# A hybrid decoder trunk on one core: batched merges of triangular inverses, one group for a pair's weighted sums, bias tiles as an input

## The chip, the cores and the metric

The kernel runs on one core of one Trainium2 chip. The metric is the time of the program on the device in microseconds (us), lower is better. Engines: TensorE (PE, its weight loads shown as PEld), VectorE (DVE), ScalarE (ACT), GpSimd (POOL) and SyncE (SP), which issues all DMA.

## What is computed

Two layers of a decoder trunk over 512 positions of width 1024, then a final RMSNorm. Each layer normalises its input, projects it once, feeds three groups of heads from the projection, multiplies each group's output with the SiLU of its own gate path, and adds one output projection to the residual. The parts that the change touches are the solve in the gated DeltaNet heads, the causal attention sweep, and the bias of the block-sparse (MoBA) heads:

```python
# gated DeltaNet, per head and chunk
L = jnp.where(strict, bc[..., :, None] * kk * decay, 0.0)
sol = lax.linalg.triangular_solve(L + jnp.eye(C), rhs, left_side=True, lower=True, unit_diagonal=True)
...
# latent attention and MoBA: softmax over past keys, weighted sum of values
p = jax.nn.softmax(logits, axis=-1)
return jnp.einsum('bhqk,bkhd->bqhd', p, v)
...
# MoBA: a T5 relative-position bias, by distance and head
rel_own = qpos[:, None] - kpos_own[None, :]
bias_own = t5_table[t5_bucket(rel_own)].transpose(2, 0, 1)[None]
l_own = jnp.einsum('bhqd,bhkd->bhqk', qi, kown) * scale
l_own = jnp.where(rel_own[None, None] >= 0, l_own + bias_own, -jnp.inf)
```

## The kernel before

The kernel's code does not issue instructions directly. `trace` (L514) records operations with the tiles that they read and write; `Plan.schedule` then runs a list scheduler with its own cost model, and `emit` writes every engine's instructions in the order found (all instructions therefore carry the line of `emit`, L485, and are told apart by their tiles). An operation's priority is its place in the recording plus a shift for its section (`TUNE`); a lower number goes first among the operations that are ready. The large projection products carry a further 1e6 (`FILL`), so that TensorE runs them only when nothing else is ready: they are called filler here. A tile takes a slot of a pool when its first operation is placed: 72 slots of 128x512 (`w`), which weights, attention tiles and others share, and 8 PSUM banks. A DMA load is placed only if ten `w` slots stay free, a weight split only if seven do. Operations inside `plan.group()` are placed as one, back to back on one engine. A `copy` goes to ScalarE or VectorE, whichever the planner finds first.

Weights come as pairs of 128x512 tiles: `wraw` is loaded, split into a high part `whi` on ScalarE and a low part `wlo` on VectorE or GpSimd, and a projection block (`fmajor`, L693) is 24 products into a PSUM bank `mm`, three for each slice of 128 rows; two split tiles make a block, so one tile of high and low parts serves 12 products. `mmt` are products with the other operand stationary (`tmajor`), the output projection among them.

**Inverses.** `N` holds L of all 4 heads, each with 4 double chunks of 128 (16 in all). Section `elim` (L934) inverts all 32x32 diagonal blocks at once on VectorE, by 31 steps over tiles of [128, 16, 32] (`row`, `xe`), to `x32` and its transpose `t32`. Section `inv` (L1204 to 1249) merges these to inverses of 64x64 blocks, head by head: a zeroed tile `X` [128, 4, 128] (`xinv`) and a zeroed `T64` [64, 4, 64]; four ScalarE copies of diagonal blocks; two GpSimd copies into `T64`; eight 32x32 products to `a2p`, two ScalarE copies to `a2`, eight products to `x12` (`x` in the trace), two signed VectorE copies into `X`, a transpose into `T64`; four 64x64 products to `a4p`, a copy to `a4`, four products to `x4p`, a signed copy into `X`, named `inv_done`. The products of a head wait for the `inv_done` of the head before. An fp32 product shows as two records. Then section `scan` of that head runs over its four double chunks: `sp` (three products on one bank), `u`, `st`, and the output `op`. Its inputs `vb`, `AT` and `qg` are made per head in section `vq` from two projection blocks.

**Attention sweep.** `attend` (L1067) is run for a pair of heads, four times in a layer. After the scores, it goes over four key blocks: for each, the weights `lg` of both heads are transposed on TensorE (`tp`) and copied to `pt`, and then a group of two products adds to `pv`, the two heads side by side in the columns of the array.

**Bias tiles.** In the first layer `t5_tiles` (L613) multiplies the 32-entry table by a one-hot array (`gdp`), scales it by 8 and fills the masked part (`gd`), writes it to DRAM (`gdd`), reads it back shifted by one per partition for each head (`hk`), turns it with an anti-diagonal (`tz`) and writes four tiles of 128x512 to DRAM (`gmd`). Both layers load these as `gmb` in MoBA's sweeps. The query is copied unscaled, and the score's scale of 0.125 is applied to the sum of score and bias.

Of the kernel before, what the change touches and what calls it, by code (L numbers as in the profile page):

```python
# [18 lines left out]
NEG = -1.0e30  # L19
# [470 lines left out]
def hybrid_trunk(  # L490
    ctx: ExitStack,
    tc: tile.TileContext,
    x_in, xt_in, ncol_in, final_norm_w, w_t1, w_v, w_f, w_o, w_uq, w_ukv, cols_in, adt_in, t5_table, trig_in, trigf_in,
    onehot_in, out,
# [12 lines left out]
          t5_table, trig_in, trigf_in, onehot_in, out)  # L507
# [6 lines left out]
def trace(plan, V, S, G, T, D,  # L514
          x_in, xt_in, ncol_in, final_norm_w, w_t1, w_v, w_f, w_o, w_uq, w_ukv, cols_in, adt_in,
          t5_table, trig_in, trigf_in, onehot_in, out):
# [87 lines left out]
    for i, j in ((0, 1), (1, 0), (2, 0), (3, 1)):  # L604
        G.memset(mask[32 * i:32 * i + 32, j:j + 1], 1.0)
    gmla = ct([P, 512], "gmla")
# [3 lines left out]
    gdd = plan.tile("dram", [4, 640], F32, "gdd")  # L610
    gmd = [plan.tile("dram", [P, 512], F32, f"gmd{h}") for h in range(4)]

    def t5_tiles():  # L613

        t5 = ht([32, 4], "t5")
        D.dma_start(t5, t5_table)
        onehot = wt([32, 512], "onehot")
        D.dma_start(onehot, onehot_in)
        gdp = g_bank("gdp")
        T.matmul(gdp[:4, :], lhsT=t5, rhs=onehot, start=True, stop=True)  # L620
        gd = wt([4, 639], "gd2")
        V.memset(gd[:, 0:127], NEG)
        V.tensor_scalar(gd[:, 127:639], gdp[:4, :], 8.0, None, op0=OP.mult)
        D.dma_start(gdd[:, 0:639], gd)
        anti = wt([P, P], "anti")
        G.memset(anti, 0.0)
        G.affine_select(anti, anti, pattern=[[1, P]], compare_op=OP.not_equal, fill=1.0,
                        base=-(P - 1), channel_multiplier=1)
# [143 lines left out]
    for l in range(L):  # L772
# [177 lines left out]
        inv_done = V.transpose(t32, x32)  # L950

        if l == 0:
            plan.section("t5")
            t5_tiles()
# [112 lines left out]
        def attend(q2, k2, gtiles, scale, v, pr, gate, ky):  # L1067
# [5 lines left out]
            for t in range(NT):  # L1073
# [7 lines left out]
                for hh in range(2):  # L1081
# [62 lines left out]
        for pr in range(2):  # L1144
# [29 lines left out]
            attend([[qs2[hh][half[hh]] for hh in range(2)], qs2], [[kh[half[hh]] for hh in range(2)], ks2], gmb, 0.125, vmb, pr, gate, 6 + pr)  # L1174
# [27 lines left out]

        for h in range(4):
            plan.section("inv")  # L1204

            X = wt([P, 4, P], "xinv")
            plan.after = [inv_done]
            G.memset(X, 0.0)
            T64 = wt([64, 4, 64], "t64")
            G.memset(T64, 0.0)  # L1210
            plan.after = ()
            for b in range(4):
                bs = slice(32 * b, 32 * b + 32)
                S.activation(X[bs, :, bs], x32[bs, 4 * h:4 * h + 4, :], AF.Copy)
            G.tensor_copy(T64[0:32, :, 0:32], t32[0:32, 4 * h:4 * h + 4, :])
            G.tensor_copy(T64[32:64, :, 32:64], t32[32:64, 4 * h:4 * h + 4, :])
            a2p = g_bank("a2p").rearrange("p (c i) -> p c i", c=4)
            plan.after = [inv_done]
            for c in range(NT):
                for q in range(2):  # L1220
                    a, b = slice(64 * q, 64 * q + 32), slice(64 * q + 32, 64 * q + 64)
                    T.matmul(a2p[b, c, 0:32], lhsT=N[h][a, c, b], rhs=t32[a, 4 * h + c, :], start=True, stop=True,
                             tile_position=(64 * q, 64 * q + 32))
            plan.after = ()
            a2 = ht([P, NT, 32], "a2")
            for q in range(2):
                b = slice(64 * q + 32, 64 * q + 64)
                S.activation(a2[b], a2p[b, :, 0:32], AF.Copy)
# [194 lines left out]
```

## Time and profile before

| | |
|---|---|
| median of 3 runs | 634.97 us (634.06 to 638.3) |
| the profiled execution, its own time | 637.48 us |
| its span, first to last instruction | 635.5 us |
| busy: TensorE, weight loads | 611.6, 493.1 us |
| busy: VectorE, ScalarE, GpSimd | 465.5, 361.9, 152.2 us |
| mean granted TensorE clock | 0.990 |
| instructions | 10493, of them 3488 matmul records |
| moved by DMA | 63.92 MB |

The profile is one execution. Times in it are microseconds from the first instruction. A busy share is covered time: matmuls overlap, so two that last 0.4 us each may start 0.23 us apart. Idle time of an engine is put down to what ended it.

### The profile page before, as it was taken

The numbers are of one execution on the slowest core, as the hardware profiler recorded it, in microseconds if no ns is written. First come the engines' busy times: TensorE is split into PE (matmuls) and PEld (weight loads), VectorE is DVE, ScalarE is ACT, GpSimd is POOL, SyncE is SP. The second block draws the span as 40 slices with busy tenths as digits, with TensorE's granted clock in tenths as the row PEclk, the third lists the DMA queues.
The fourth block names the chain that finished last, engine by engine and source line by source line (L and its number), as shares of the span: only waits on it lengthen the run. The fifth ranks groups of instructions, "written<-read, shape, count | busy, mean of one in ns | idle before, by whom it ended". The sixth has DMA issues, their size and how long they took to land.

```text
span 635.5 us, 10493 instructions
## 1 busy us (share of the span) xinstructions
PE 611.6 (96%) x3488; PEld 493.1 (78%) x3488; DVE 465.5 (73%) x1351; ACT 361.9 (57%) x948; POOL 152.2 (24%) x177
## 2 busy tenths in 40 slices
PE   8989999999999999999999899899999999999994
PEld 7767878877767887888898788688777688778884
DVE  6589878999857767734572888658999787786265
ACT  7887974624768545423455698447346976344032
POOL 2526503341403122000023141124402422030000
PEclk9999999998999999999999999989999999999998
DMA  8890341111123422350663112510012214214002
GB/s 313 301 331 18 116 131 51 51 50 51 52 67 118 134 68 96 101 195 0 195 214 114 57 45 85 166 34 1 18 51 84 67 68 150 76 57 166 0 35 100
DMA packets 36190, 63.92 MB, mean 101 GB/s; under 512 B 4644, under 2 KB 7428, under 8 KB 36136
## 3 DMA queue, kind: packets, MB, share of 16 engines
q1 hardware_dynamic: 36136, 63.26, 30.5%
q8 instruction: 27, 0.44, 0.3%
q14 instruction: 27, 0.22, 0.1%
HBM read 57.94 MB, written 5.30 MB: 100 GB/s over the span
## 4 chain that ended last, share of the span: by engine, by line
PE 62%; DVE 19%; ACT 8%; issue 5%; DMA 3%; POOL 2%; SPq 0%; POOLq 0%; ACTq 0%; DVEq 0%
PE mm L485 22%; PE mmt L485 19%; DVE row L485 6%; PE sp L485 3%; DVE xe L485 2%; PE tp L485 2%; PE pv L485 2%; PE op L485 2%; ACT n L485 1%; DVE mm L485 1%; DVE ks L485 1%; PE qkp L485 1%; DVE vs L485 1%; ACT lg L485 1%; DVE wlo L485 1%
## 5 line engine op out<-in xcount | busy, mean ns | idle before, releaser
L485 POOL TENSOR_TENSOR wlo<-wraw,whi 128x512 fp32r<-128x512 f32 x72 | 95.9, 1346 | 290.9 <-ACT whi L485 216.9
L485 PE MATMUL mm<-hy_hi,whi 128*128 128x512 f32 x384 | 155.1, 408 | 0.4 <-DVE vs L485 0.4
L485 PE MATMUL mm<-hy_lo,whi 128*128 128x512 f32 x384 | 154.9, 406 | 0.0
L485 PE MATMUL mm<-hy_hi,wlo 128*128 128x512 f32 x384 | 154.1, 406 | 0.0
L485 ACT ACTIVATE whi<-wraw 128x512 fp32r<-128x512 f32 (+1 forms) x152 | 88.7, 619 | 5.2 <-DMA wraw<-in_w_f_dram 4.4
L485 PEld LDWEIGHTS mm<-hy_hi,whi 128*128 128x128 f32 x384 | 72.9, 190 | 14.6 <-issue 1.3
L485 PEld LDWEIGHTS mm<-hy_hi,wlo 128*128 128x128 f32 x384 | 73.0, 190 | 14.0 <-issue 0.2
L485 PEld LDWEIGHTS mm<-hy_lo,whi 128*128 128x128 f32 x384 | 72.8, 190 | 14.0 <-issue 0.6
L485 DVE TENSOR_TENSOR wlo<-wraw,whi 128x512 fp32r<-128x512 f32 (+1 forms) x80 | 57.1, 738 | 3.2 <-ACT whi L485 3.1
L485 ACT ACTIVATE lg<-lg,nm 128x128 f32<-128x128 f32 (+3 forms) x64 | 35.3, 555 | 4.5 <-DVE nm L485 4.3
L485 PE MATMUL mmt<-whi,hy_hi 128*128 128x256 f32 (+1 forms) x128 | 34.4, 330 | 0.1
L485 PE MATMUL mmt<-wlo,hy_hi 128*128 128x256 f32 (+1 forms) x128 | 33.7, 324 | 0.0
L485 PE MATMUL mmt<-whi,hy_lo 128*128 128x256 f32 (+1 forms) x128 | 33.6, 323 | 0.0
L485 DVE STREAM_SHUFFLE row<-n 128x496 f32<-128x496 f32 (+30 forms) x62 | 28.9, 470 | 0.3
L485 DVE TENSOR_TENSOR xe<-xe,row 128x496 f32<-128x496 f32 (+30 forms) x62 | 26.2, 423 | 0.6
L485 PEld LDWEIGHTS mmt<-whi,hy_hi 128*128 128x128 f32 x128 | 24.5, 193 | 2.2 <-ACT whi L485 1.4
L485 ACT ACT_TABLE_LOAD x18 | 23.1, 1283 | 3.8 <-DMA ncol<-in_ncol_dram 3.5
L485 DVE TENSOR_TENSOR row<-row,xe 128x496 f32<-128x496 f32 (+30 forms) x62 | 25.0, 404 | 0.0
L485 PEld LDWEIGHTS mmt<-whi,hy_lo 128*128 128x128 f32 x128 | 24.1, 189 | 1.1 <-issue 0.7
L485 PEld LDWEIGHTS mmt<-wlo,hy_hi 128*128 128x128 f32 x128 | 24.6, 193 | 0.5
L485 DVE TENSOR_TENSOR mm<-mm,rrow 128x512 f32<-128x512 f32 x32 | 22.2, 693 | 3.8 <-PE mm L485 3.8
L485 PE MATMUL tp<-ident,lg 128*128 128x128 f32 x160 | 23.3, 277 | 0.0
(688 smaller groups left out, 1307.2 us busy)
## 6 DMA issues: line engine op xcount, KB each, us to landing
wraw<-in_w_f_dram SPq DMA_DIRECT2D x96, 256.0 KB, 3.5
wraw<-in_w_o_dram SPq DMA_DIRECT2D x32, 256.0 KB, 3.0
xt<-in_xt_dram SPq DMA_DIRECT2D x16, 256.0 KB, 4.7
wraw<-in_w_t_dram SPq DMA_DIRECT2D x16, 212.0 KB, 3.7
x<-in_x_dram SPq DMA_DIRECT2D x8, 256.0 KB, 4.9
wraw<-in_w_v_dram SPq DMA_DIRECT2D x8, 256.0 KB, 5.8
rb<-gcd SPq DMA_DIRECT2D x8, 256.0 KB, 4.7
y<-rd SPq DMA_DIRECT2D x16, 128.0 KB, 3.5
```

The lines of the kernel that those rows point to most:

```text
L485: o.insts.append(getattr(engines[o.eng], method)(*args, **kw))
```

## The change

Three edits. The merges of the inverses are recorded for all four heads at once, ahead of the first scan: `X` is one constant tile [128, 16, 128] and `T64` [64, 16, 64], zeroed once at the start and reused by both layers; each step handles 16 double chunks, its products in one group (two groups of eight where a bank holds eight), and copies into `T64` may go to ScalarE or VectorE instead of GpSimd. In `attend`, the transposes of all key blocks come first and the eight products into `pv` are one group. The bias tiles arrive as an input array in their final layout, so `t5_tiles` and its DRAM tiles go; the query is scaled by 0.125 when it is copied, and the score's scale becomes 1.

```diff
+    X = ct([P, 16, P], "xinv")
+    G.memset(X, 0.0)
+    T64 = ct([64, 16, 64], "t64")
+    G.memset(T64, 0.0)
...
-    gdd = plan.tile("dram", [4, 640], F32, "gdd")
-    gmd = [plan.tile("dram", [P, 512], F32, f"gmd{h}") for h in range(4)]
-
-    def t5_tiles():
...
-        T.matmul(gdp[:4, :], lhsT=t5, rhs=onehot, start=True, stop=True)
...
-        for h in range(4):
-            hk = wt([P, 512], "hk")
-            D.dma_start(hk, gdd.strided(h * 640, [[1, P], [1, 512]]))
-            tp = g_bank("tz")
-            with plan.group():
-                for b in range(4):
-                    T.transpose(tp[:, b * P:(b + 1) * P], hk[:, (3 - b) * P:(4 - b) * P], anti)
-            tz = wt([P, 512], "tz")
-            V.tensor_copy(tz, tp)
-            D.dma_start(gmd[h], tz)
...
+            pts = [[], []]
             for k in range(NT):
                 n = P * (NT - k)
-                pts = []
                 for hh in range(2):
...
-                    pts.append(pt)
-                with plan.group():
+                    pts[hh].append(pt)
+            with plan.group():
+                for k in range(NT):
                     for hh in range(2):
                         h = 2 * pr + hh
                         T.matmul(pv[hh * 64:hh * 64 + 64, k * P:], lhsT=v[k // 2][:, k % 2, h * 64:(h + 1) * 64],
-                                 rhs=pts[hh][:, :n], start=(k == 0), stop=(k == NT - 1), tile_position=(0, hh * 64))
+                                 rhs=pts[hh][k][:, :P * (NT - k)], start=(k == 0), stop=(k == NT - 1),
+                                 tile_position=(0, hh * 64))
...
-                S.activation(qs2[hh][half[hh]], p[half[hh]], AF.Copy)
+                S.activation(qs2[hh][half[hh]], p[half[hh]], AF.Copy, scale=0.125)
...
-                V.tensor_tensor(qs2[hh][other], p[own], qs2[hh][own].bitcast(F32), op=OP.subtract)
+                V.scalar_tensor_tensor(qs2[hh][other], p[own], 0.125, qs2[hh][own].bitcast(F32), op0=OP.mult, op1=OP.subtract)
...
-                gmb_done = [D.dma_start(g, gmd[2 * pr + hh])]
+                gmb_done = [D.dma_start(g, t5_in[2 * pr + hh])]
...
+        plan.section("inv")
+        low, high = (slice(0, 32), slice(64, 96)), (slice(32, 64), slice(96, 128))
+        for b in range(4):
+            bs = slice(32 * b, 32 * b + 32)
+            S.activation(X[bs, :, bs], x32[bs], AF.Copy)
+        for bs in (low[0], high[0]):
+            copy(T64[bs, :, bs], t32[bs])
+        a2p = g_bank("a2p").rearrange("p (c i) -> p c i", c=16)
+        with plan.group():
+            for i in range(16):
+                for a, b in zip(low, high):
+                    T.matmul(a2p[b, i, :], lhsT=N[i // 4][a, i % 4, b], rhs=t32[a, i, :], start=True, stop=True,
+                             tile_position=(a.start, b.start))
+        a2 = wt([P, 16, 32], "a2")
+        for b in high:
+            S.activation(a2[b], a2p[b], AF.Copy)
+        x12 = g_bank("x12").rearrange("p (c i) -> p c i", c=16)
+        with plan.group():
...
+        for a, b in zip(low, high):
+            V.tensor_scalar(X[a, :, b], x12[a], -1.0, None, op0=OP.mult)
+        V.transpose(T64[32:64, :, 0:32], X[0:32, :, 32:64])
+        a4 = []
+        for g in range(2):
+            p = g_bank("a4p").rearrange("p (c i) -> p c i", c=8)
+            with plan.group():
+                for i in range(8):
+                    T.matmul(p[64:128, i, :], lhsT=N[2 * g + i // 4][0:64, i % 4, 64:128], rhs=T64[:, 8 * g + i, :],
+                             start=True, stop=True, tile_position=(0, 64))
+            a4.append(wt([P, 8, 64], "a4"))
+            copy(a4[g][64:128], p[64:128])
+        for g in range(2):
+            p = g_bank("x4p").rearrange("p (c i) -> p c i", c=8)
+            with plan.group():
...
+            V.tensor_scalar(X[0:64, 8 * g:8 * g + 8, 64:128], p[0:64], -1.0, None, op0=OP.mult)
+
         for h in range(4):
-            plan.section("inv")
-
-            X = wt([P, 4, P], "xinv")
-            plan.after = [inv_done]
-            G.memset(X, 0.0)
-            T64 = wt([64, 4, 64], "t64")
-            G.memset(T64, 0.0)
...
-                T.matmul(sp[:, 1, :], lhsT=X[:, c, :], rhs=x1, start=True, stop=True)
+                T.matmul(sp[:, 1, :], lhsT=X[:, 4 * h + c, :], rhs=x1, start=True, stop=True)
```

The host's layout function builds the bias array by picking table entries by distance, with the mask's value where the key lies ahead.

## Rows read from the trace of the kernel before

**Rows 1.** The page's first part: busy time, share of span, instructions of each engine.
```profile
PE 611.6 (96%) x3488; PEld 493.1 (78%) x3488; DVE 465.5 (73%) x1351; ACT 361.9 (57%) x948; POOL 152.2 (24%) x177
```
**Rows 2.** The chain that ended last, merged pieces: start us, us, what.
```profile
91.28 2.30 PE pv L485 x16
...
302.49 16.71 PE mmt L485 x72
```
**Rows 3.** Timeline of TensorE, bias tiles: start, us, engine line op out<-in [idle before <-releaser].
```profile
23.65 1.02 PE L485 MATMUL gdp<-onehot,t 32*4 32x512 f32 x2
...
27.02 0.39 PE L485 MATMUL mm<-hy_hi,whi 128*128 128x512 f32 x1
...
30.90 0.40 PE L485 MATMUL mm<-hy_lo,whi 128*128 128x512 f32 x1
32.14 0.63 PE L485 MATMUL tz<-anti,hk 128*128 128x128 f32 x4 [0.84 <-DMA hk<-gdd]
...
37.25 0.48 PE L485 MATMUL mm<-hy_hi,wlo 128*128 128x512 f32 x1
```
**Rows 4.** Busy time by stretch: stretch, its length, engines (xcount), clock, DMA share, GB/s.
```profile
31.00:37.30 6.30, 3.30 (x22) 2.19 (x20) 5.38 (x18) 4.63 (x18) 5.52 (x7) 1.00 0.90 233
...
115.00:145.00 30.00, 27.85 (x143) 23.14 (x142) 29.35 (x76) 10.72 (x20) 12.74 (x10) 1.00 0.18 53
...
530.00:587.00 57.00, 56.63 (x325) 45.16 (x324) 42.84 (x124) 26.20 (x84) 9.00 (x7) 1.00 0.33 111
```
**Rows 5.** The same of tile wlo alone: PE, PEld, DVE, POOL.
```profile
17.00:31.00 14.00, 5.33 (x20) 3.76 (x20) 2.50 (x3) 6.59 (x4) 1.00 0.88 296
```
**Rows 6.** Timeline of TensorE, 191 to 196, one head's merges among filler.
```profile
191.32 0.40 PE L485 MATMUL mm<-hy_hi,whi 128*128 128x512 f32 x1
191.65 0.68 PE L485 MATMUL a4p<-t,N 64*64 64x64 f32 x8
192.25 0.50 PE L485 MATMUL mm<-hy_lo,whi 128*128 128x512 f32 x1
192.59 0.39 PE L485 MATMUL mm<-hy_hi,wlo 128*128 128x512 f32 x1
...
195.12 0.44 PE L485 MATMUL a2p<-t,N 32*32 32x32 f32 x16
195.49 0.50 PE L485 MATMUL mm<-hy_hi,whi 128*128 128x512 f32 x1
```
**Rows 7.** Tiles a2p and xinv: count, ns min/median/max, first and last start.
```profile
L485 PE MATMUL a2p<-t,N x128: 190/191/213, 167.8 to 526.8; 32*32 32x32 f32 x128
...
L485 ACT ACTIVATE xinv<-x x32: 292/306/312, 169.0 to 528.6; 32x128 f32<-32x128 f32 x32
...
L485 POOL MEMSET xinv<- x8: 518/524/532, 164.5 to 525.7; 128x512 f32 x8
```
**Rows 8.** Timeline of GpSimd, its first weight splits.
```profile
21.86 2.97 POOL L485 TENSOR_TENSOR wlo<-wraw,whi 128x512 fp32r<-128x512 f32 x2 [16.47 <-ACT whi L485]
```
**Rows 9.** Timeline of TensorE, a pair's weighted sums and what starts next.
```profile
173.99 1.08 PE L485 MATMUL pv<-pt,vmoba 128*64 128x512 f32 x4
175.03 0.65 PE L485 MATMUL a4p<-t,N 64*64 64x64 f32 x8
...
187.42 0.44 PE L485 MATMUL pv<-pt,vmoba 128*64 128x128 f32 x4
187.79 0.49 PE L485 MATMUL sp<-x,xinv 128*128 128x128 f32 x2
```
**Rows 10.** Waits of SP's queue: for what, us in total, times, longest.
```profile
SPq L485 <- PE tp L485: 41.8, 7, 23.2
```
**Rows 11.** Timelines in layer 1: the last inverse (VectorE), the last head's scan (TensorE).
```profile
535.72 0.42 DVE L485 TENSOR_SCALAR xinv<-x4p 64x256 f32<-64x256 f32 x1 [2.53 <-PE x4p L485]
...
566.51 0.38 PE L485 MATMUL sp<-vb,xinv 128*128 128x128 f32 x2
```

More of the change, by code (lines that the diff above doesn't have):

```diff
@@ L492, in hybrid_trunk @@
     tc: tile.TileContext,
-    x_in, xt_in, ncol_in, final_norm_w, w_t1, w_v, w_f, w_o, w_uq, w_ukv, cols_in, adt_in, t5_table, trig_in, trigf_in,
-    onehot_in, out,
+    x_in, xt_in, ncol_in, final_norm_w, w_t1, w_v, w_f, w_o, w_uq, w_ukv, cols_in, adt_in, t5_in, trig_in, trigf_in, out,
 ):
@@ L506, in hybrid_trunk @@
     trace(plan, V, S, G, T, D, x_in, xt_in, ncol_in, final_norm_w, w_t1, w_v, w_f, w_o, w_uq, w_ukv, cols_in, adt_in,
-          t5_table, trig_in, trigf_in, onehot_in, out)
+          t5_in, trig_in, trigf_in, out)
     plan.schedule()
@@ L515, in trace @@
           x_in, xt_in, ncol_in, final_norm_w, w_t1, w_v, w_f, w_o, w_uq, w_ukv, cols_in, adt_in,
-          t5_table, trig_in, trigf_in, onehot_in, out):
+          t5_in, trig_in, trigf_in, out):
     L = w_t1.shape[0]
@@ L609, in trace @@
                     fill=NEG, base=0, channel_multiplier=1)
-    gdd = plan.tile("dram", [4, 640], F32, "gdd")
-    gmd = [plan.tile("dram", [P, 512], F32, f"gmd{h}") for h in range(4)]
-    def t5_tiles():
[L615 to L619, printed above, removed]
-        T.matmul(gdp[:4, :], lhsT=t5, rhs=onehot, start=True, stop=True)
[L621 to L628, printed above, removed]
-        for h in range(4):
-            hk = wt([P, 512], "hk")
-            D.dma_start(hk, gdd.strided(h * 640, [[1, P], [1, 512]]))
-            tp = g_bank("tz")
-            with plan.group():
-                for b in range(4):
-                    T.transpose(tp[:, b * P:(b + 1) * P], hk[:, (3 - b) * P:(4 - b) * P], anti)
-            tz = wt([P, 512], "tz")
-            V.tensor_copy(tz, tp)
-            D.dma_start(gmd[h], tz)
     def copy(o, i, scale=None):
@@ L949, in trace @@
         t32 = wt([P, 16, 32], "t32")
[L950 to L954, printed above, removed]
+        V.transpose(t32, x32)
         plan.section("mlap")
@@ L1173, in trace @@
             plan.section("moba")
-            attend([[qs2[hh][half[hh]] for hh in range(2)], qs2], [[kh[half[hh]] for hh in range(2)], ks2], gmb, 0.125, vmb, pr, gate, 6 + pr)
+            attend([[qs2[hh][half[hh]] for hh in range(2)], qs2], [[kh[half[hh]] for hh in range(2)], ks2], gmb, 1.0, vmb, pr, gate, 6 + pr)
         plan.section("vq")
@@ new lines, in trace @@
+        a2 = wt([P, 16, 32], "a2")
[3 more added lines that the diff above has]
+        with plan.group():
+            for i in range(16):
+                for a, b in zip(low, high):
+                    T.matmul(x12[a, i, :], lhsT=a2[b, i, :], rhs=x32[b, i, :], start=True, stop=True,
+                             tile_position=(b.start, a.start))
+        for a, b in zip(low, high):
+            V.tensor_scalar(X[a, :, b], x12[a], -1.0, None, op0=OP.mult)
@@ L1252, in trace @@
+        for g in range(2):
+            p = g_bank("x4p").rearrange("p (c i) -> p c i", c=8)
+            with plan.group():
+                for i in range(8):
+                    T.matmul(p[0:64, i, :], lhsT=a4[g][64:128, i, :], rhs=X[64:128, 8 * g + i, 64:128],
+                             start=True, stop=True, tile_position=(64, 0))
+            V.tensor_scalar(X[0:64, 8 * g:8 * g + 8, 64:128], p[0:64], -1.0, None, op0=OP.mult)
+        for h in range(4):
             plan.section("scan")
@@ L1371, in _shape_constants @@
     bucket = np.where(n < 16, n, np.minimum(large, 31))
-    onehot = np.zeros((32, seq), np.float32)
-    onehot[bucket, np.arange(seq)] = 1.0
     cos, sin = trig[0].T, trig[1].T
     trigf = np.stack([np.tile(np.concatenate([cos, cos]), (4, 1)), np.tile(np.concatenate([-sin, sin]), (4, 1))])
-    return trig.reshape(2, 4, P, 16).transpose(2, 0, 1, 3), trigf, onehot
+    return trig.reshape(2, 4, P, 16).transpose(2, 0, 1, 3), trigf, bucket
 def layout(inp):
@@ L1389, in layout @@
     ukv = inp["mla_w_ukv"].reshape(L, P, 4, 128)
-    trig, trigf, onehot = _shape_constants()
+    trig, trigf, bucket = _shape_constants()
+    dist = 384 + np.arange(P)[:, None] - np.arange(512)[None, :]
+    t5 = np.where(dist >= 0, inp["t5_table"].T[:, bucket[np.maximum(dist, 0)]], np.float32(NEG))
     return {
@@ L1401, in layout @@
         "adt": np.stack([inp["gdn_A_log"], inp["gdn_dt_bias"]]),
-        "t5_table": inp["t5_table"],
-        "trig": trig, "trigf": trigf, "onehot": onehot,
+        "t5": t5.astype(np.float32),
+        "trig": trig, "trigf": trigf,
     }
```

39 lines of the change are left out of this document (removed).

## The prediction

> **What bounds the kernel now.** I read the page first, then the chain of work that ended last, then TensorE's order of work around each place that the change touches, then busy time by stretch. On the page TensorE is busy 96% of the span [rows 1]. "Busy" needs care, since matmuls overlap: what counts is how soon the next one can start. In the chain 72 matmuls on 512 columns take 16.71 us, 0.232 each [rows 2], and 14 filler products start one after another between 27.02 and 30.90, mostly 0.23 apart, while each lasts 0.40 [rows 3]. So I price TensorE by the distance from one start to the next, which I call a slot, and not by durations. By stretch [rows 4], TensorE is covered for 56.63 of 57 us in 530 to 587, where the last scans and sums run. There is one hole: between 31.0 and 37.3 it is covered for 3.30 of 6.30 us. The reader is to see an engine that always has a filler product to run (the planner puts the large products behind all other work), and therefore a kernel whose time is the sum of TensorE's slots. An instruction that goes saves its slot, if the filler behind it is there.
>
> **Bias tiles.** Sixteen transposes and one small product go, and with them four reads of 256 KB, four writes of as much, three small transfers and six VectorE operations. In [rows 3] the last filler product before the first transposes starts at 30.90 and holds its slot to 31.13; the next unbroken stretch begins at 37.25. In these 6.12 us three products ran (3 x 0.232 = 0.70): 5.42 us are the transposes and the waits ahead of them, 0.84 us in front of the first four. The small product at 23.65 holds about 0.9 us (two records, 1.02 with the tail of the last). Together 6.3 us. Is filler there to take the place? In 17 to 31 VectorE and GpSimd begin seven low halves of weights [rows 5]; leaving out two for work before it and work unfinished, five halves at 12 products each are 60, and 14 had started by 31. So yes. The low bound is that only the slots go and the waits return elsewhere: 4 x 0.38 + 0.9 = 2.4 (0.38 is what remains of the 0.63 of four transposes, less the tail that overlaps the next product). I take 6.3, since the supply is several times what the hole holds. SP's queue loses the four writes that wait for VectorE's copies of the transposes; what stood behind them, the weights of the latent projections among it, can only come earlier. The reads of the bias tiles by the block-sparse attention stay: same size, same queue, another source.
>
> **Inverses.** The same matmuls, 96 a layer, in 6 groups instead of 16. What a group costs beside its work is seen in [rows 6]: the product before it holds 0.33 (191.32 to 191.65) and the one behind it 0.34 (192.25 to 192.59) instead of 0.23, so 0.21 for the two edges. A group of 64x64 matmuls (eight records) holds 0.60 between them, a group of 32x32 ones (16 records) 0.37 (195.12 to 195.49). With edges that is 0.81 and 0.58; eight of each a layer, 11.1 us. After: four groups of 16 records hold at most 2 x 0.60 + 0.21 = 1.41 each, 5.6. The 32x32 records start (0.44 - 0.19) / 15 = 0.017 apart, with the 0.19 of one record [rows 7]; 64 of them hold 64 x 0.017 + 0.10 of drain + 0.21 = 1.4, two groups 2.8. That is 8.4 a layer, 2.7 saved, 5.4 in both layers. Bounds: 3, if the edges stay with the neighbours (other narrow work may then stand there); 9, if the drains of the 64x64 groups go too and those groups that are now interrupted pay no second edges. I take 6, near the value of the rows. The evictions shrink in number: 32 copies of diagonal blocks of 0.306 us on ScalarE [rows 7] become 8 of four times the width, 1.2 us each at the very most, so between nothing and 9.8 - 4.2 = 5.6 goes there. Copies into the transposed tile move from GpSimd to ScalarE or VectorE, four in all, each at most 1.2. All of it has TensorE's filler for cover; without it, the chain is a rival below. The two memsets go, once, to the start of GpSimd's queue, and GpSimd stands idle for 16.47 us before 21.86 [rows 8]: at 0.524 us for 512 elements [rows 7] both need some 3 us (3072 elements). No cost there; were GpSimd not idle, the first low halves would come these 3 us later.
>
> **Weighted sums.** Four groups of a pair become one. The 512-column group holds 1.04 us (173.99 to 175.03), the 128-column one 0.37 (187.42 to 187.79) [rows 9]: 384 columns are 0.67, so 0.15 of each group is fixed, and 0.21 of edges come to it. 24 groups go, 24 x 0.36 = 8.6, if all stood apart; they don't, for in the chain one whole pair runs unbroken in 2.30 us [rows 2], as one group of the new kind should (1280 columns, 2.23, and a drain). I take half, 4; bounds 2 and 6. The price is that eight transposed tiles live to the end of the sweep instead of two (a rival, below), and that the whole sum waits for the last copy; what stands behind it on TensorE is ordered by the planner to be filler.
>
> **Scale in the query copy.** ScalarE's copy takes a constant factor, VectorE's subtraction becomes multiply-and-subtract; eight of each. I price both at nothing, since neither reads or writes more. From above: were it a whole further pass, at 0.42 us for 256 columns [rows 11] some 0.84 each, VectorE would have 6.7 us more, which TensorE's filler covers, and which would be 6.7 us of time only where there is none; from below nothing.
>
> **Sum.** 6.3 + 6 + 4 = 16.3. The profiled execution took 637.48 us (span 635.5 and 2.0 around it), so 621.2; it stands 2.5 above the median of the runs, 634.97, and at the median's level this is 618.7. Forecast 619. Its own range: low terms 2.4 + 3 + 2 = 7.4, so 627.6; high terms 6.3 + 9 + 6 = 21.3, so 613.7, and some two less if the 2 MB of early transfers that go let later weights land sooner.
>
> **Rivals.**
>
> *The merged chain waits for its evictions.* Between its four products stand two 32-row copies, two signed copies and a transpose, two copies and two signed copies, each for the whole batch: with 0.306 us for 128 columns [rows 7] and 0.42 for 256 [rows 11] and no gain from width, 2.4 + 2.4 + 1.2 + 1.7 + 1.7 = 9.4 us a layer; half of that, with the fixed part paid once, is nearer. If TensorE stood idle for half, 4.7 a layer, 9.4 come back: 628. Against it: in [rows 6] TensorE runs filler right behind a group while the copy goes on. Chance 0.14.
>
> The Trainium skill speaks for this rival ("TensorEngine Tiling (Array Packing)", PSUM Bottleneck): tiling speeds up TensorE but not the copies out of PSUM, which may then become the limit. By that rule the inverse part brings nothing and the time would be 625 or above; by the rows the copies run beside filler, and the trace agrees with the rule only where filler is short.
>
> *VectorE's elimination gives part back.* In 115 to 145 VectorE is busy 29.35 of 30 us [rows 4], and the inverses cannot begin before it is done. If the time freed ahead of it (the bias tiles) only brings TensorE earlier to the end of its filler there, 6.3 come back: 625. Against it: what comes before the elimination is TensorE's work too, and moves with it. Chance 0.13.
>
> *Slower: weights starve.* Eight transposed tiles of 128x512 are held to the one group instead of two, six more out of a pool of 72 from which the weight tiles come too, and a load is not placed while fewer than ten would stay free. SP's queue already waits 41.8 us in 7 places for transposes to release a tile [rows 10]. If each of the eight sweeps holds weights back so long that TensorE has no filler for 5 us, 40 us come on top of 619: 659. It decides from some 2.8 us a sweep (22.6 us: the 16.3 and 1% of the time). For it: those waits. Against it: the inverses' tiles, two a head, leave that pool, and there are five halves of weights ahead in [rows 5]. Chance 0.12.
>
> That a late batch holds up the scans I leave out: the last inverse is ready at 536.13, and the last head's scan begins at 566.51 [rows 11], 30 us of cover.
>
> **How the numbers follow.** Forecast 0.60, the three rivals 0.14, 0.13 and 0.12, 0.01 for what I don't see. A measurement of this kernel can tell about 1%: the lines are 628.6 and 641.3. Faster: 0.60, most of the elimination's case and a little of the evictions' case, which lies on the line: 0.69. Within 1%: 0.19. Slower: 0.12. The range 611 to 634 leaves out the slower case and some 0.06 at its edges.
>
> **What would show it.** TensorE covered without a hole between 25 and 45 us: first term. One run of 64 small records for each of the two 32-wide products in a layer, and no idle time of several us around them: second. Unbroken runs of 16 records for the weighted sums, about 2.3 us long: third. It is wrong if the covered share of TensorE falls in the new trace where scans and attention stand, with waits for weight splits or for copies ahead of its work; or if its slots shrink as said and the span does not.

## The result and the profile after

| | before | after |
|---|---|---|
| median | 635.03 us (634.06 to 638.3) | 618.22 us (616.14 to 621.02) |
| ratio, 95% interval | | 0.9726 (0.968 to 0.9772) |
| profiled execution, its span | 637.48, 635.5 us | 618.93, 617.2 us |
| mean granted clock of it | 0.990 | 0.991 |
| moved by DMA | 63.92 MB | 61.72 MB |

The change saves 16.8 us, 2.7%. The forecast was 619.0, but two of its three terms were wrong, in opposite directions; most of this section and the next ones is about that. Runs more than 1.5% above the fastest of their kernel (one in e1, three in e10) are left out of the ratios.

From the page of after, to set beside [rows 1]: span and instructions, then busy time of each engine.

```profile
span 617.2 us, 10314 instructions
...
PE 592.1 (96%) x3470; PEld 488.4 (79%) x3470; DVE 462.0 (75%) x1315; ACT 354.6 (57%) x908; POOL 166.9 (27%) x161
```

TensorE is as full as before (96%), with 19.5 us less of covered time and 18.3 less of span. The distances from each matmul's start to the next add up to 624.7 us before and 606.1 after. That sum runs from the first start to the last and holds the waits too, so it follows the span by itself and proves nothing; it is of use only where it is split by tile, as further down.

Timeline of TensorE in after, layer 0's merges (compare [rows 6 and 7]): start, us, engine line op out<-in, form, records [idle before <-releaser].

```profile
172.48 1.20 PE L485 MATMUL a2p<-t,N 32*32 32x32 f32 x64
...
176.17 1.19 PE L485 MATMUL x<-x,a 32*32 32x32 f32 x62 [0.37 <-ACT a L485]
...
179.90 2.08 PE L485 MATMUL a4p<-t,N 64*64 64x64 f32 x32
181.92 1.11 PE L485 MATMUL x4p<-xinv,a 64*64 64x64 f32 x16
...
183.69 1.14 PE L485 MATMUL x4p<-xinv,a 64*64 64x64 f32 x16
```

The 64 records of each 32-wide product run together (those of `x` as 2 and 62, with a wait of 0.37 us between), both 64-wide groups of `a4p` back to back. The whole chain of layer 0 takes TensorE from 172.48 to 184.8; before, with four heads one after another, its products stood between 167.75 and 201.9.

The chain that ended last, after: start, us, what (compare [rows 2]).

```profile
85.92 2.31 PE pv L485 x16
...
188.47 2.30 PE pv L485 x16
...
205.19 2.31 PE pv L485 x16
```

The weighted sums of a pair run unbroken in all eight sweeps. And the start of the program, to set beside the first line of [rows 4], by stretch: length, busy PE, PEld, DVE, ACT, POOL (xcount), granted clock, DMA share, GB/s.

```profile
31.00:37.30 6.30, 6.30 (x30) 5.10 (x30) 6.16 (x24) 6.30 (x20) 4.12 (x5) 1.00 1.04 381
37.30:47.00 9.70, 6.74 (x33) 5.29 (x32) 9.35 (x34) 7.58 (x12) 5.69 (x5) 0.97 0.26 88
47.00:67.00 20.00, 18.09 (x87) 15.07 (x86) 14.72 (x32) 15.94 (x35) 10.17 (x8) 0.84 0.02 6
```

The last two stretches before:

```profile
37.30:47.00 9.70, 9.70 (x52) 7.93 (x51) 9.00 (x37) 9.03 (x16) 0.00 (x0) 1.00 1.04 392
47.00:67.00 20.00, 19.45 (x100) 15.27 (x98) 18.86 (x44) 16.15 (x33) 12.93 (x11) 1.00 0.20 68
```

The hole at 31 to 37.3 is closed: 6.30 of 6.30 us. But behind it there is a new one, 2.96 us without a matmul in 37.3 to 47, and in 47 to 67 the clock is granted at 0.84 of full speed on average, that is at half for some 6.3 of the 20 us. Before, both of these stretches had a clock of 1.00 and were covered for 9.70 of 9.70 and 19.45 of 20 us.

### The profile page after: what moved, and what is told of

It reads as the page before. It is cut to its first block, busy times and chain, and to the rows that moved or that the text cites. A ratio compares the mean times of both kernels' runs of the same rounds, so it can differ in the third digit from the quotient of the medians.

```text
span 617.2 us, 10314 instructions
## 1 busy us (share of the span) xinstructions
PE 592.1 (96%) x3470; PEld 488.4 (79%) x3470; DVE 462.0 (75%) x1315; ACT 354.6 (57%) x908; POOL 166.9 (27%) x161
## 2 busy tenths in 40 slices
DMA packets 34931, 61.72 MB, mean 100 GB/s; under 512 B 4448, under 2 KB 7232, under 8 KB 34880
## 4 chain that ended last, share of the span: by engine, by line
PE 67%; DVE 17%; ACT 7%; DMA 3%; issue 3%; POOL 1%; SPq 1%; ACTq 0%; POOLq 0%; DVEq 0%
PE mm L485 26%; PE mmt L485 18%; DVE row L485 5%; PE pv L485 3%; PE sp L485 3%; PE tp L485 3%; DVE xe L485 2%; PE op L485 2%; DMA wraw<-in_w_t_dram 2%; ACT n L485 2%; DVE qs L485 1%; PE kkp L485 1%; ACT whi L485 1%; ACT scr L485 1%; DVE kl L485 1%
## 5 line engine op out<-in xcount | busy, mean ns | idle before, releaser
L485 POOL TENSOR_TENSOR wlo<-wraw,whi 128x512 fp32r<-128x512 f32 x83 | 111.1, 1350 | 272.9 <-ACT whi L485 198.8
L485 PE MATMUL mm<-hy_hi,whi 128*128 128x512 f32 x384 | 150.4, 403 | 0.8 <-DVE qs L485 0.8
L485 PE MATMUL mm<-hy_lo,whi 128*128 128x512 f32 x384 | 149.8, 401 | 0.0
L485 PE MATMUL mm<-hy_hi,wlo 128*128 128x512 f32 x384 | 149.8, 402 | 0.0
L485 DVE TENSOR_TENSOR wlo<-wraw,whi 128x512 fp32r<-128x512 f32 (+1 forms) x69 | 51.5, 765 | 5.3 <-ACT whi L485 5.2
L485 POOL TENSOR_TENSOR ylo<-y,yhi 128x512 fp32r<-128x512 f32 x8 | 10.9, 1362 | 60.0 <-ACT yhi L485 60.0
L485 ACT ACTIVATE gate<-gate 128x512 f32<-128x512 f32 x16 | 10.1, 635 | 27.8 <-DVE gate L485 27.8
```

What stands on the lines that cost most here:

```text
L485: o.insts.append(getattr(engines[o.eng], method)(*args, **kw))
```

## The experiments

Each median is set against the runs of the kernel before beside it (635.2 to 635.4). First, every part by itself.

**e1_bias_only**: the bias tiles as an input and the scale in the query copy, nothing else.

```diff
-    def t5_tiles():
...
-                S.activation(qs2[hh][half[hh]], p[half[hh]], AF.Copy)
+                S.activation(qs2[hh][half[hh]], p[half[hh]], AF.Copy, scale=0.125)
...
-                gmb_done = [D.dma_start(g, gmd[2 * pr + hh])]
+                gmb_done = [D.dma_start(g, t5_in[2 * pr + hh])]
```

> Of the three edits only the bias tiles (with the query's scale). Slot theory (a kernel's time is the sum of TensorE's slots; filler takes what is freed): 6.3 us below before, about 628.7, and no hole between 31 and 37. Rival, the hole only moves (the freed 5.4 us of waiting come back as a wait for another operand in the same stretch): 2.4 below, about 632.6, with a new hole of several us before 70.

Measured: 632.45 us, ratio 0.9954 (0.9934 to 0.9974): 2.9 us, not 6.3. The hole has moved, as the rival said: TensorE, PE alone (busy, clock, DMA share, GB/s), and its longest wait.

```profile
17.00:67.00 50.00, 44.14 (x226) 1.00 0.52 183
```
```profile
45.29 0.52 PE L485 MATMUL latp<-ident,lt 128*128 128x128 f32 x3 [3.02 <-DVE lt L485]
```

**e2_inv_only**: the merges batched, nothing else. (The two constant tiles need room; the pool of small tiles has 54 instead of 56, here and in e5, e6, e9 and e11.)

```diff
-        for h in range(4):
-            plan.section("inv")
...
+        plan.section("inv")
+        low, high = (slice(0, 32), slice(64, 96)), (slice(32, 64), slice(96, 128))
```

> Of the three edits only the merged inverses (with two small tiles fewer, so that the constants fit). Slot theory: 6 us below before, about 629, bounds 3 and 9. Rival, the merged chain waits for its evictions: within 1 us of before, with idle time of TensorE ahead of the products of the merge. Rival, the order: one change of the program gives another plan for everything, and the time moves by some us in either direction, whatever the slots do.

Measured: 621.21 us, ratio 0.9774 (0.9752 to 0.9796): 14.2 us, more than twice the forecast, and outside its bounds of 3 to 9. TensorE's timeline shows that the products run as they do in after:

```profile
175.55 1.20 PE L485 MATMUL x<-x,a 32*32 32x32 f32 x64
179.07 2.05 PE L485 MATMUL a4p<-t,N 64*64 64x64 f32 x32
180.97 2.14 PE L485 MATMUL x4p<-xinv,a 64*64 64x64 f32 x32
```

**e3_pv_only**: the group of a pair's weighted sums, nothing else.

```diff
+            pts = [[], []]
             for k in range(NT):
...
-                with plan.group():
+            with plan.group():
+                for k in range(NT):
                     for hh in range(2):
```

> Of the three edits only the weighted sums in one group. Slot theory: 4 us below before, about 631, bounds 2 and 6. Rival, eight held tiles starve the weights: above before, with TensorE waiting for weight splits in the sweeps.

Measured: 632.19 us, ratio 0.9958 (0.9941 to 0.9975): 3.2 us, forecast 4. The three parts alone sum to 20.3 us, together they bring 16.8.

**e4_replan**: the kernel before, with one constant of the planner's cost model moved, so that the same operations come out in another order. It asks how much a new order alone moves the time.

```diff
-LAT_SAME = {"PE": 0.0, "DVE": 115.0, "ACT": 130.0, "POOL": 100.0, "SP": 0.0}
+LAT_SAME = {"PE": 0.0, "DVE": 117.0, "ACT": 130.0, "POOL": 100.0, "SP": 0.0}
```

> The kernel before with one number of the planner's cost model changed (2 ns in VectorE's latency to itself): the same operations, another order on every engine. Slot theory: within 1.5 us of before, since the slots are the same. Rival, the order: it moves by 3 us or more, and then single parts of a few us can't be told from a new plan.

Measured: 635.71 us, ratio 0.9995 (0.9976 to 1.0014). One draw is not a distribution, but 14.2 us is far above what reordering alone did here. For parts of 3 us one draw is too little: e7 and e9 below, which change only an order and where two tiles lie, come out 2.2 and 2.5 us slower, so a new order may be worth nearly as much as e1 or e3.

**e11_without_bias**: the change without its bias part (merges and sums only). By e2 and e3 the two should bring 17.3.

```diff
-    x_in, xt_in, ncol_in, final_norm_w, w_t1, w_v, w_f, w_o, w_uq, w_ukv, cols_in, adt_in, t5_in, trig_in, trigf_in, out,
+    x_in, xt_in, ncol_in, final_norm_w, w_t1, w_v, w_f, w_o, w_uq, w_ukv, cols_in, adt_in, t5_table, trig_in, trigf_in,
+    onehot_in, out,
...
-                gmb_done = [D.dma_start(g, t5_in[2 * pr + hh])]
+                gmb_done = [D.dma_start(g, gmd[2 * pr + hh])]
```

> The change without its bias tiles: merged inverses and the weighted sums in one group. By the parts alone (14.2 and 3.2) 617.6 if they add up, and then the bias tiles bring nothing to the whole change, which is at 618.2. If the bias tiles bring their 2.9 in the whole change too, 621.

Measured: 616.17 us, ratio 0.971 (0.9683 to 0.9736): 19.0 us, more than the 17.3 of the two parts. That is 2 us below the full change by the medians; the intervals overlap (after: 0.968 to 0.9772). So in the full change the bias part brings nothing that can be measured.

Why not? In after's trace VectorE, in 42 to 46 us, shows what TensorE's wait hangs on:

```profile
42.52 2.29 DVE L485 SCALAR_TENSOR_TENSOR kl<-kpp,mask,kh 64x512 fp32r<-64x512 f32 x3
44.82 1.27 DVE L485 TENSOR_SCALAR lt<-lt,rl_y 128x256 f32<-128x256 f32 x5
```

and TensorE, the last product before the hole and the first behind it:

```profile
41.96 0.39 PE L485 MATMUL mm<-hy_lo,whi 128*128 128x512 f32 x1
45.31 0.52 PE L485 MATMUL latp<-ident,lt 128*128 128x128 f32 x3 [2.96 <-DVE lt L485]
```

The last product ends at 42.35; the next work in TensorE's order, the transposes of `lt`, waits until VectorE has made `lt`, and VectorE runs three subtractions `kl` (2.29 us) first. Before, `lt` came first there, 1.4 us earlier:

```profile
43.38 1.91 DVE L485 TENSOR_SCALAR lt<-lt,rl_y 128x256 f32<-128x256 f32 x8
45.32 1.53 DVE L485 SCALAR_TENSOR_TENSOR kl<-kpp,mask,kh 64x512 fp32r<-64x512 f32 x2
```

Two experiments follow this up.

**e7_late_bias**: the kernel before, with the bias tiles' section of lower priority, so that their transposes come later.

```diff
-        "mlap": -224.9, "inv": 1348.7, "decay": -382.7, "t5": 149.2, "out": -161.4,
+        "mlap": -224.9, "inv": 1348.7, "decay": -382.7, "t5": 900.0, "out": -161.4,
```

> The kernel before with the section of the bias tiles put later in the planner's order (shift 900 instead of 149.2), so that their transposes don't stand in front of filler while their reads are under way; the slots stay. By the prediction's first term the waits, 3.9 us of the 6.3, go: about 631.5. Rival, the hole only moves to the next operand that is late in the first 70 us: within 1 us of before.

Measured: 637.62 us, ratio 1.0038 (1.0016 to 1.0059), 2.2 us slower. By stretch, PE alone (busy, clock, DMA share, GB/s):

```profile
17.00:31.00 14.00, 10.48 (x51) 1.00 0.97 331
31.00:37.30 6.30, 6.30 (x20) 0.73 0.63 192
```

The hole of [rows 4] is gone from 31 to 37.3, and 3.52 us of hole stand in 17 to 31 instead, with a slow clock behind it. Most of that hole is still the bias part's own: its small product waits for its one-hot operand.

```profile
30.54 1.01 PE L485 MATMUL gdp<-onehot,t 32*4 32x512 f32 x2 [2.17 <-DMA onehot<-in_onehot_dram]
```

So e7 does not show where the hole goes when the bias part's waits are gone; e1 does.

**e12_bias_order**: the full change, with one dependence more: the `kl` subtractions may not start before `lt`'s chain (`lat_done`) is through.

```diff
+            plan.after = [lat_done]
             V.scalar_tensor_tensor(kl[h][half], kpp[half], m, kh[h][half].bitcast(F32), op0=OP.mult, op1=OP.subtract)
+            plan.after = ()
```

> The changed kernel, with VectorE's four subtractions of the rotary keys held until the latent transposes are done. In the changed kernel three of them stand in front of the scaling of the latents, and TensorE waits 2.96 us for that at 42 to 45. If that wait is what the bias tiles' term lacks: some 3 us below the changed kernel, 615. Rival, the next operand is late instead, or the new order costs elsewhere: 618 or above.

Measured: 615.51 us (614.59 to 616.53), ratio 0.9689 (0.9667 to 0.9712): 2.7 us below after by the medians, the fastest version tried; the intervals overlap, and e11's too. TensorE over the whole stretch 17 to 67 us in before, after, e11 and e12, in this order (busy, clock, DMA share, GB/s):

```profile
17.00:67.00 50.00, 46.45 (x232) 1.00 0.65 215
```
```profile
17.00:67.00 50.00, 44.47 (x210) 0.93 0.48 172
```
```profile
17.00:67.00 50.00, 46.43 (x236) 1.00 0.66 221
```
```profile
17.00:67.00 50.00, 46.84 (x229) 0.97 0.54 183
```

Uncovered time plus what the clock falls short of full speed, an estimate from these lines: 3.55 us before, 5.53 + 0.07 x 50 = 9.0 after, 3.57 in e11, 3.16 + 0.03 x 50 = 4.7 in e12. The slots of the bias part's own matmuls, which e11 has and the others of the change have not, are 2.5 us in the trace of before. So this stretch should make after 9.0 - 3.57 - 2.5 = 2.9 slower than e11 (medians: 2.05), and e12 1.4 faster (0.7). The clock's part of this comes from one execution each: after's four runs have mean granted clocks of 0.984 to 0.996 and e11's six 0.984 to 0.994, so the two kernels don't differ in it. Without it the waits alone say the same: over the whole span after is uncovered for 25.1 us, e11 for 20.9 and e12 for 21.1, and 4.2 - 2.5 = 1.7 us is near the 2.05 by which e11 is below after. What e12 gets is not a closed hole: it waits too, now for a gate's operand, 2.85 us at 40 to 43. What it avoids is what came behind: in 47 to 67 it is covered for 19.91 of 20 us at 0.97.

```profile
43.17 0.37 PE L485 MATMUL gp<-gg,tri 128*128 128x16 f32 x2 [2.85 <-DVE gg L485]
```

Second, what makes the merges worth 14.2 us? Three candidates besides the groups: the wide copies, the constant tiles, and that the heads no longer wait for one another.

**e5_narrow_groups**: e2 with the products grouped by head, 16 groups a layer, copies as wide as before.

```diff
-        with plan.group():
-            for i in range(16):
-                for a, b in zip(low, high):
+        for h in range(4):
+            with plan.group():
+                for i in range(4 * h, 4 * h + 4):
+                    for a, b in zip(low, high):
```

> The merged inverses alone, as in the run with only that edit, but TensorE's products stand in groups of one head again (16 groups a layer instead of 6); the copies and signed copies between them stay as wide as the batch. Slot theory: the 10 groups more cost their drains and edges, 2.7 us a layer by the working of the prediction, so 5 to 6 of the 14.2 us come back: about 627. Rival, the count of copies: what the edit brings beyond 5.5 us comes from fewer instructions on ScalarE, VectorE and GpSimd, so little of the gain goes: about 622 to 624. Rival, the batch: heads no longer wait for one another's merges, 621.

Measured: 621.87 us, ratio 0.9792 (0.9759 to 0.9825), 13.5 us. The edit did not do what it was for:

```profile
168.99 1.20 PE L485 MATMUL a2p<-t,N 32*32 32x32 f32 x64
...
176.54 1.20 PE L485 MATMUL x<-x,a 32*32 32x32 f32 x64
```

Where nothing else is more urgent, the planner puts the four groups back to back anyway. So it says that the recording of one group is not needed; on what edges cost it says nothing.

**e6_narrow_copies**: e2 with one group for each step, and each copy cut into pieces of one head (those into `T64` on GpSimd again).

```diff
         for b in high:
-            S.activation(a2[b], a2p[b], AF.Copy)
+            for c in range(0, 16, 4):
+                S.activation(a2[b, c:c + 4], a2p[b, c:c + 4], AF.Copy)
```

> The merged inverses alone, with one group of products a step as in the edit, but every copy, signed copy and transpose between them is cut into parts of one head again (46 instructions a layer instead of 15), and the copies into the transposed tile go to GpSimd as before. Slot theory: the products' slots are as in the edit, so 621. Rival, the count of copies: the gain beyond 5.5 us goes, about 629.

Measured: 622.87 us, ratio 0.9802 (0.977 to 0.9834), 12.5 us. Narrow copies cost at most a microsecond or two. In tile `a2p`'s lines of e6 and of after (ns min/median/max) they are 16 of 258 ns against 4 of 590:

```profile
L485 ACT ACTIVATE a<-a2p x16: 252/258/270, 171.9 to 491.0; 32x128 f32<-32x128 f32 x16
```
```profile
L485 ACT ACTIVATE a<-a2p x4: 588/590/590, 174.9 to 491.1; 32x512 f32<-32x512 f32 x4
```

**e9_constant_tiles**: the kernel before, with `X` and `T64` as slices of constant tiles zeroed once, head by head otherwise.

```diff
-            X = wt([P, 4, P], "xinv")
-            plan.after = [inv_done]
-            G.memset(X, 0.0)
...
+            X = XC[:, 4 * h:4 * h + 4, :]
+            T64 = TC[:, 4 * h:4 * h + 4, :]
```

> The kernel before with one thing of the merged inverses alone: the inverses and their transposed tiles are constant tiles, zeroed once at the start; the merges still run head by head, each after the one before, with narrow products and copies. Theory A, the gain beyond the products' own slots comes from the tiles (no memsets in GpSimd's queue that wait for a free tile, eight tiles more for weights): 5 us or more below before, under 630. Theory B, it comes from the products of all heads being ready at once: within 2 us of before.

Measured: 637.71 us, ratio 1.0031 (1.001 to 1.0052). The constant tiles alone bring nothing: this kernel is 2.5 us slower, by them or by the new order.

**e10_heads_first**: the kernel before, with the merges of all heads recorded ahead of the scans and not waiting for one another, but neither batched nor grouped.

```diff
+        first_done = inv_done
         for h in range(4):
...
-            plan.after = [inv_done]
+            plan.after = [first_done]
...
+        for h in range(4):
             plan.section("scan")
```

> The kernel before with the merges of all four heads recorded ahead of the scans and no longer waiting for one another; tiles, memsets, products and copies stay as before, one head each. Theory A (the tiles): within 2 us of before. Theory B (ready at once, so that TensorE finds another head's products where it waited for a copy): most of the 14 us of the merged form, 622 to 626.

Measured: 668.23 us by the median of all six runs (658.24 to 671.91, mean granted clock 0.941 to 0.961), ratio 1.045 (1.0394 to 1.0507), that is 29 us by the runs counted there. TensorE in e10, 180 to 215 us (the profiled execution is the longest of the six): the heads' products mix record by record, TensorE runs out of other work, waits, and then is covered without a gap at half clock.

```profile
180.19 0.22 PE L485 MATMUL a2p<-t,N 32*32 32x32 f32 x2
180.21 0.22 PE L485 MATMUL x<-x,a 32*32 32x32 f32 x3
...
183.24 0.31 PE L485 MATMUL x<-x,a 32*32 32x32 f32 x8 [0.87 <-ACT a L485]
184.51 0.65 PE L485 MATMUL a4p<-t,N 64*64 64x64 f32 x4 [0.95 <-DVE vs L485]
```
```profile
180.00:184.00 4.00, 2.00 (x64) 1.00 0.30 80
...
188.00:212.00 24.00, 24.00 (x103) 0.50 0.18 56
```
```profile
180.00:215.00 35.00, 32.49 (x224) 0.56 0.24 76
...
510.00:560.00 50.00, 46.95 (x353) 0.73 0.17 55
```

The clock's shortfall in the last two stretches is 0.44 x 35 + 0.27 x 50 = 28.9 us, in a profiled span that is 34.4 longer than the one of before; there the granted clock was 1.00 in 180 to 215 and in 510 to 560. So e10 does not price its edit by itself: most of its loss is clock, and what it would take at full clock was not measured. It shows only that letting the heads' merges mix, record by record, did not bring the gain.

Last, is TensorE the bound, as all of this assumes?

**e8_more_products**: the full change, with a fourth product per slice in the gates' projections (the low part of the weight by the low part of the input, a term that the reference does not need): 64 more on 512 columns, 64 x 0.232 = 14.8 us of slots.

```diff
+            if B_GZ <= b:
+                T.matmul(p, lhsT=lo, rhs=hy_lo[:, k, :], start=False, stop=False)
```

> The changed kernel with 64 more products of 512 columns on TensorE (the product of the two low parts in the eight gate blocks of the DeltaNet heads), a known load of 64 x 0.232 = 14.8 us of slots as filler. Slot theory: 14.8 us above the changed kernel's 618.2, so 633. Rival, TensorE has room (its weight loads are busy 79%): less than half of it, under 626.

Measured: 633.61 us (631.03 to 639.39), ratio 0.999 to before (0.9958 to 1.0021): 15.4 us more than after by the medians, 14.6 by the profiled spans.

```profile
PE 608.2 (96%) x3534; PEld 501.0 (79%) x3534; DVE 463.1 (73%) x1324; ACT 356.9 (56%) x908; POOL 157.5 (25%) x154
```

A microsecond of slots added as filler is a microsecond of time, to within the some 3.5 us that the two kernels' intervals leave open, with TensorE's share at 96% as before.

## Why the prediction came out right, and where it was wrong

**The bound: right for what is added.** "A kernel whose time is the sum of TensorE's slots" is what e8 shows: 14.8 us of slots cost 15.4. That a slot or a wait that goes is saved in full is another matter, and the bias tiles show that it need not be.

**Bias tiles: 2.9 alone and nothing measurable in the whole, not 6.3.** The step that failed is "Is filler there to take the place? ... So yes". The count of filler was right and the question was wrong. The tile of loaded weights, busy on DVE, ACT and POOL in 17 to 67 us, before and after:

```profile
17.00:67.00 50.00, 5.37 (x5) 13.58 (x22) 13.40 (x9) 1.00 0.65 215
```
```profile
17.00:67.00 50.00, 6.27 (x6) 12.90 (x22) 13.90 (x10) 0.93 0.48 172
```

ScalarE makes 22 high halves in this stretch in both. How they are used up is seen by counting the large `mm` products begun: 38 by 42.5 us before and 65 after, but 61 and 72 by 57 us. Seven were left for the 14.5 us behind the hole, where before had 23: what fills the hole at 31 was not spare but the work of 42. (Further on the 22 are no limit: by 67 us after has begun 85 and e12 95.) SP shows why no more arrives. Its longest wait in 30 to 75 us after (before: 14.9):

```profile
SPq L485 <- DVE gct L485: 25.7, 1, 25.7
```

After, SP issues the last weight load of this stretch at 35.6 us, then stands at the write of `gct`, and the next weight load goes out at 67.4; before, the last was at 46.2 and the next at 64.1. "What stood behind them ... can only come earlier" is true, and the loads ran ten microseconds ahead; but TensorE used them ten microseconds earlier too, and then met the chain of small steps on VectorE (`lt`), which had not become shorter and, with `kl` in front, began 1.4 us later than before. The low bound of the forecast, 2.4 ("only the slots go and the waits return elsewhere"), was the right reading: e1 measured 2.9. Over the whole span TensorE is uncovered for 23.8 us before and 24.0 in e1, so all of the waits came back, and what is left is the bias part's own slots, 2.5 us. (Runs with a mean granted clock of 0.996 or more say the same: medians of 633.6 us before and 630.7 in e1.) In the full change even that went, to the waits behind 42 us (e11, e12); what the half clock adds there differs from execution to execution. With intervals of after, e11 and e12 that overlap, this last step is argued from the traces, not shown by the times. That an earlier load would have closed the hole was not tried.

**Inverses: 14.2, not 6.** The step that failed is the sum "8.4 a layer, 2.7 saved". Its 5.4 us in both layers were 4.2 for edges (32 groups down to 12, at 0.21) and 1.2 for the groups' own slots (15.5 us down to 14.3). By the distances between starts, the four kinds of products hold 17.9 us before and 12.4 in e2: 5.5 of their own, not 1.2. And the edges were counted too low, and the waits ahead of the products not at all. Two places in TensorE's timeline before:

```profile
187.79 0.49 PE L485 MATMUL sp<-x,xinv 128*128 128x128 f32 x2
188.21 0.44 PE L485 MATMUL a2p<-t,N 32*32 32x32 f32 x16
...
195.83 0.39 PE L485 MATMUL mm<-hy_lo,whi 128*128 128x512 f32 x1
196.66 0.73 PE L485 MATMUL x<-x,a 32*32 32x32 f32 x16 [0.44 <-ACT a L485]
```

TensorE turns from other work to a merge product 43 times before, since the groups are broken up, and 6 times in e2. Ahead of 31 of the 43 turns a product holds its slot about 0.09 us longer than its like (a scan's `sp` 0.205 for 0.112, as at 187.79); ahead of the other 12 it is more, at most 0.60 (the `mm` at 195.83, where TensorE waits for a copy): 6.8 us in all, and 0.7 in e2. Behind most turns a product holds 0.06 to 0.10 us more (`mm` 0.34 for 0.23, `tp` 0.165 for 0.109), which makes another 2 us or so. So 5.5 + 6.1 + some 2 is near the 14.2, and over half of it stood in the neighbours. Counting the large products alone misses this (132 `mm` products have a slot of 0.26 to 0.35 us before, and 132 in e2, where other narrow work stands beside them), since only 13 of the 43 turns come from an `mm` product.

By tile, the same is seen in the stretches from the end of VectorE's elimination to the end of a layer's mixing (layer 0: 164.6 to 300.6 us before, 164.8 to 293.8 in e2; layer 1: the last 142.8 us of the span against 136.4). They are 13.4 us shorter, and the slots fell by:

| matmuls | us less, both layers |
|---|---|
| the four merge products | 5.5 |
| `sp` and `op`, the scans | 3.0 |
| `mm`, the waits ahead of narrow work (12 slots over 0.35 us, now 4) | 2.3 |
| `yp`, transposes of the gated outputs | 1.9 |
| `tp`, transposes in the attention sweep | 1.2 |

The rest comes to 0.5 us the other way. Before, four chains of four dependent products stood one after another among scans and sweeps, and each product or part of one was a turn; after, one chain is over by 184.8 us and the scans that follow have all inverses ready. The bounds did not hold this, because "all of it has TensorE's filler for cover" was taken for the waits of before, too. In these stretches the uncovered time fell by only 1.6 us (10.3 to 8.7): the rest stood in slots that were too long while TensorE counted as busy, which its covered share hides. What this part rests on is only partly separated: wide copies (e6), the single recorded group (e5) and constant tiles (e9) are each not it, and e10 can't tell, for its clock. The number of turns goes with the time over these kernels (40 to 43 in before, e4 and e9, at 635 to 638 us; 6 in e2 and 9 in e5 and e6, at 621 to 623), but no run changed it by itself.

**Weighted sums: 3.2, forecast 4.** The unbroken run takes 2.30 to 2.31 us as foreseen. Runs of `pv` fell from 19 to 8, so 11 breaks went, about the half of 24 that the forecast took. `pv`'s own slots fell from 20.32 to 18.44 us, 0.17 a break, near the 0.15 of the forecast's fixed part; the other 1.3 us of the 3.2 stand beside them and are less than 11 x 0.21 = 2.3 of edges. The price of an edge seems to be the term that was too large; but 1.3 us is less than a new order alone may move, so this is not shown.

**The sum.** Against the parts alone the forecast had 3.4 too much for the bias tiles, 0.8 too much for the sums and 8.2 too little for the inverses, and it did not see the 3.5 that the parts lose together: 16.3 - 3.4 - 0.8 + 8.2 - 3.5 = 16.8. By the medians the loss is the bias part's: without it the other two bring 19.0, not 17.3. The total was right, the working was not; that the errors cancel is luck.

**The rivals.** *The merged chain waits for its evictions* fell: in after the copies of four times the width take 0.59 us against 0.258, those of the diagonal blocks 0.63 against 0.306 (not 1.2), TensorE's waits ahead of `x` come to 0.4 us, and e6, with narrow copies, is not faster. The limit that the Trainium skill names, copies out of PSUM once tiling has sped TensorE up ("TensorEngine Tiling (Array Packing)", PSUM Bottleneck), is not seen in these runs. *VectorE's elimination gives part back* was the right kind of reason at the wrong place: it was VectorE that took back the time freed by the bias part, but with the small steps at 42 us, well ahead of the elimination; in 115 to 145 us TensorE is covered for 29.09 of 30 us after, 27.85 before. *Weights starve* fell: e3, which holds the eight tiles, is faster. In after GpSimd's weight splits wait 20.4 us in two places for such a tile, and the time falls all the same.

**The smaller claims.** The zeroing of the constant tiles at the start costs nothing visible in e2 or after; the scale edit had no run apart from the bias part, but its price of nothing holds in the traces: ScalarE's eight copies take 0.594 us each and VectorE's eight subtractions 0.689 in both. The first sign asked for (no hole between 25 and 45 us) failed, the second and third were there. The stated way of being wrong, "its slots shrink as said and the span does not", is what happened to the bias part alone.

## What to carry to other kernels

Where filler covers an engine, ask not whether enough of it is there at the hole but whether it is spare: here 65 of the 72 large products begun by 57 us had gone by 42.5, and the hole opened again there. For an engine that takes its work in a fixed order, price a serial chain of small products by the turns to it and back, counted in the trace, and by the waits ahead of each, not by the chain's own slots alone; here over half of the gain stood in the products beside it, under a covered share of 96%. And measure each part alone: three terms that miss can still add up.

## What the runs showed of the hardware that was not expected

- TensorE's granted clock can stay at its lower level (0.50, 1.2 of 2.4 GHz) while the trace shows the engine covered: in e10 for 24.00 of 24 us in 188 to 212, where it ran scans, transposes, 64-wide products and four weighted sums, and none of the large projection products. It fell at 184.0, among waits of up to 0.95 us in 179 to 184.5. In after it fell at 46.5, just behind a wait of 2.96 us, and at 60.1, among waits of 0.85 and 0.83.
- A few microseconds of waiting can therefore cost twice, but need not: in 17 to 67 us after loses 5.53 us uncovered and some 3.5 more to the clock, and e1, with a wait of 3.02 us in the same place, 5.86 us uncovered and nothing to the clock. The clock also differs between executions of one kernel: in after's four runs the time follows its mean (616.14 us at 0.996, 617.51 at 0.994, 618.93 at 0.991, 621.02 at 0.984).
- A copy of 32x512 takes 0.59 us on ScalarE where 32x128 takes 0.258: four times the width costs 2.3 times as much.
